# Two of the four sums of weight quarters in each feed-forward block: from VectorE and GpSimd to accumulating DMAs

## The chip, the cores and the metric

The kernel runs on one core of a Trainium2 chip. The metric is the device time of one execution in microseconds (us), the median of three. TensorE (PE) multiplies matrices, VectorE (DVE) and ScalarE (ACT) work on tiles in the on-chip memory, GpSimd (POOL) does so more slowly, and SyncE (SP) issues the loads. Each engine takes its instructions in the order in which the program lists them.

## The reference

A transformer encoder of four layers on one sequence of 512 tokens of width 1024, in float32. A layer is an attention of one of three kinds and then a gated feed-forward part; what is changed stands in the latter:

```
def swiglu(h, w_gu, w_out):
    gu = h @ w_gu
    return (jax.nn.silu(gu[..., :FFN_DIM]) * gu[..., FFN_DIM:]) @ w_out

for i in range(DEPTH):
    ...
    x = x + mix
    x = x + swiglu(rms_norm(x, ffn_norm[i]), f_w_gu[i], f_w_out[i])
```

FFN_DIM is 2816, which is 22 tiles of 128 columns.

## The kernel before

Each float32 matrix is split into a high and a low part (`split`: ACT copies the high part, DVE subtracts it from the source), and a product is three matmuls: high by high, high by low, low by high (`mm3`). In each layer's feed-forward part (`ffn`) the first 4 of the 22 column tiles are computed as they are (`whole`); the other 18, four times 18 = 72 in the kernel, are **blocks** of a fast scheme for 2 by 2 blocks (`quartered`): the activations are combined once per layer (`quarters`), and of the weights of a block four quarters a11, a12, a21, a22 (each 128 partitions by 512 elements, 256 KB) are loaded, from which four sums are made,

    s1 = a21 + a22,   s2 = a11 + s1,   s4 = a12 + s2,   s3 = a11 + a21

so that seven products of 12 matmuls each (256 columns) take the place of eight. The program makes them in the order 5, 2, 1, 3, 6, 7, 4; product 5 reads s1, 3 reads s4, 6 reads s2 and 7 reads s3. Products 1, 3, 6, 7 and 4 build up in three PSUM tiles; after products 1, 6, 7 and 4 DVE takes an intermediate sum out of PSUM (`tmp<-b,tmp`, 128 by 256), and the next product into the same tile waits for that.

Where things lie: the buffer `raw` has eight quarters, 0 to 7. s1, s4, s2, s3 of every block lie in quarters 3, 4, 5 and 6: there is one set of them, used by one block after the other. The loaded a11, a12, a22, a21 of an even block lie in quarters 0, 1, 2 and 7 of `raw`, those of an odd one in `rt` (two), `acc` and `rb`. The split parts have two sets of buffers: even blocks use `whi`, `wlo`, odd ones for the sums `g` and for a11, a12, a22 `whi`, `wlo` as well. In DVE's rows the split of s1 and s4 is the first `128x1024` of a block that reads `raw` (its high part is made by ACT), the split of s2 and s3 is the second; when the first is over, quarters 3 and 4 are free for the next block.

Between the blocks' products PE multiplies the hidden tiles of the phase before by the down weights (matmuls of 512 columns on `xh`, `xl` or `s`; two output tiles a block).

What sets the order: nothing is issued by hand. `Plan` records every operation with a cost and a lag, `run` makes twelve list schedules of the whole program, and the best one fixes the order of the instructions on each engine. The hardware then goes through these fixed orders and waits where an operand is not there. All loads are issued by SP through one queue (`dma`, line 406).

Of the kernel before, what the change touches and what calls it, by code (L numbers as in the profile page):

```python
# [10 lines left out]
ALU = mybir.AluOpType  # L11
# [9 lines left out]
FFN = 2816  # L21
# [157 lines left out]
class Plan:  # L179
# [222 lines left out]
    def dma(self, out, in_, nbytes):  # L402

        nc = self.nc
        val = lambda s: s.ap() if isinstance(s, View) else s
        return self.op("sp", max(475.0, nbytes / 359.0), lambda: nc.sync.dma_start(out=val(out), in_=val(in_)),
                       [in_] if isinstance(in_, View) else [], [out] if isinstance(out, View) else [],
                       lag=2000.0)

# [146 lines left out]
class Net:  # L558
# [272 lines left out]
    def quartered(self, ring, wg, f, xq, sets):  # L831


        p = self.p
        raw = self.raw.buf
        q = lambda b, n, c=1: Region(b, 512 * n, [128, 4 * c, 128])

        if f % 2:
            a21, a22, a11, a12 = q(self.rb, 0), q(self.acc, 0), q(self.rt, 0), q(self.rt, 1)
            plain = [(0, 2, q(self.rt, 0, 2)), (2, 1, a22)]  # L840
        else:
            a21, a22, a11, a12 = q(raw, 7), q(raw, 2), q(raw, 0), q(raw, 1)
            plain = [(0, 3, q(raw, 0, 3))]
        s1, s4, s2, s3 = (q(raw, n) for n in range(3, 7))
        for v, half, c0 in ((a21, 0, FFN), (a22, 1, FFN), (a11, 0, 0), (a12, 1, 0)):
            src = wg[512 * half:512 * (half + 1), c0 + 128 * f:c0 + 128 * (f + 1)].rearrange("(k p) m -> p k m", p=128)
            p.dma(v.all, src, 1 << 18)
        (ha, la), (hb, lb) = sets

        def split(h, l, at, n, src):  # L850
            v = slice(4 * at, 4 * (at + n))
            p.act(h[:, v, :], src.all)
            p.tt(l[:, v, :], src.all, h[:, v, :].bits(F32), ALU.subtract)

        p.tt(s1.all, a21.all, a22.all, ALU.add)
        p.tt(s2.all, a11.all, s1.all, ALU.add)
        p.tt(s4.all, a12.all, s2.all, ALU.add)
        split(hb, lb, 0, 2, q(raw, 3, 2))
        for at, n, src in plain:
            split(ha, la, at, n, src)  # L860
        p.tt(s3.all, a11.all, a21.all, ALU.add, eng="pool")
        split(hb, lb, 2, 2, q(raw, 5, 2))

        place = {1: (ha, la, 0), 2: (ha, la, 1), 4: (ha, la, 2), 5: (hb, lb, 0), 3: (hb, lb, 1), 6: (hb, lb, 2), 7: (hb, lb, 3)}
        n = slice(0, T // 2)
        x, y, z = (self.psum(ring)[:, n] for _ in range(3))
        c1, c2 = slice(0, T // 2), slice(T // 2, T)

        def product(n, out, first):
            h, l, at = place[n]  # L870
            for k in range(NT):
                self.mm3(out, h[:, 4 * at + k, :], l[:, 4 * at + k, :], *xq[n, k], first and k == 0, k == NT - 1, more=not first)

        s, o, t, u = self.tmp.new([128, T]), self.tmp.new([128, T]), self.tmp.new([128, T]), self.tmp.new([128, T // 2])
        product(5, y, True)
        p.act(t[:, c2], y)
        product(2, x, True)
        p.act(t[:, c1], x)
        product(1, z, True)
        p.tt(s[:, c1], z, t[:, c1], ALU.add)  # L880
        product(3, y, False)
        p.act(u.all, y)
        product(6, z, False)
        p.tt(s[:, c2], z, u.all, ALU.add)
        p.act(s.all, s.all, ACTF.Silu)
        product(7, z, False)
        p.tt(o[:, c2], z, t[:, c2], ALU.add)
        p.tt(o[:, c2], o[:, c2], s[:, c2], ALU.mult)
        product(4, z, False)
        p.tt(o[:, c1], z, s[:, c1], ALU.mult)  # L890
        return o
# [752 lines left out]
```

## Time and profile before

| | |
|---|---|
| median of 3 runs | 2734.08 us (2733.46 to 2734.75) |
| the profiled execution | 2733.77 us, of which its span (first to last instruction) 2732.0 us |
| PE busy | 2703.5 us, 99% of the span |
| DVE, ACT, POOL busy | 73%, 51%, 23% |
| granted TensorE clock, mean | 0.997 of full speed |
| read from HBM | 230.66 MB |

Busy shares are averages over attention and feed-forward parts. "Idle before" in a row is the time that the engine waited ahead of an instruction, with what ended the wait.

### The profile page before, as it was taken

What the parts mean: (1) busy time and instruction counts of PE and PEld (TensorE: products, weight loads), DVE (VectorE), ACT (ScalarE), POOL (GpSimd) and SP (SyncE); (2) the same over time, 40 slices, a digit from 0 to 9 for tenths busy, and PEclk for the clock granted to TensorE, in tenths of its full rate; (3) what the DMA queues carried; (4) which work ended last, traced back from release to release, by engine and by line L of the source; (5) the groups of instructions that cost most, each with busy time, mean ns of one, the idle gap of its engine ahead of it and who ended that gap; (6) DMA issues with size and microseconds to landing.
All of it is one profiled execution on the core that took longest, in us unless ns stands there. A gap on an engine that the chain in (4) does not pass through costs nothing.

```text
span 2732.0 us, 43805 instructions
## 1 busy us (share of the span) xinstructions
PE 2703.5 (99%) x16757; PEld 2330.3 (85%) x16757; DVE 1983.5 (73%) x3599; ACT 1382.0 (51%) x2577; POOL 619.3 (23%) x462
## 2 busy tenths in 40 slices
PE   8999999999999999999999999999999999999999
PEld 6778899997777899988888888889998778889998
DVE  7876897756666887765767585688776778688774
ACT  5555444445874544445454545454444555454442
POOL 2432211003642211021312122221101433211001
PEclk9999999999999999999999999999999999999999
DMA  4222343332112343232232322324323212224322
GB/s 145 64 69 62 93 127 106 93 88 60 43 55 86 93 123 93 86 110 80 71 79 63 94 71 79 98 85 120 97 81 117 70 39 81 86 86 117 104 74 66
DMA packets 474975, 235.79 MB, mean 86 GB/s; under 512 B 47935, under 2 KB 471694, under 8 KB 474766
## 3 DMA queue, kind: packets, MB, share of 16 engines
q1 hardware_dynamic: 474766, 233.00, 29.8%
q8 instruction: 131, 2.15, 0.3%
q14 instruction: 78, 0.64, 0.1%
HBM read 230.66 MB, written 2.29 MB: 85 GB/s over the span
## 4 chain that ended last, share of the span: by engine, by line
PE 95%; DVE 2%; ACT 1%; DMA 1%; issue 0%; POOL 0%; SPq 0%; DVEq 0%; POOLq 0%; ACTq 0%
PE b L261 86%; PE b L304 4%; PE b L282 2%; PE b L271 2%; PE b L293 0%; ACT s L328 0%; DVE tmp L341 0%; DVE s L341 0%; DMA raw<-in_a_w_qkv 0%; DVE wlo L341 0%; DVE raw L341 0%; DVE tmp L396 0%; DVE tmp L352 0%; ACT tmp L328 0%; DMA s<-in_x 0%
## 5 line engine op out<-in xcount | busy, mean ns | idle before, releaser
L261 PE MATMUL b<-s,whi 128*128 128x256 f32 (+1 forms) x4000 | 869.4, 313 | 3.5 <-ACT s L328 1.4
L261 PEld LDWEIGHTS b<-s,whi 128*128 128x128 f32 x4000 | 662.1, 191 | 57.6 <-issue 2.1
L261 PE MATMUL b<-s,wlo 128*128 128x256 f32 (+1 forms) x2000 | 623.6, 312 | 0.9 <-DVE wlo L341 0.9
L328 ACT ACTIVATE whi<-raw 128x1024 fp32r<-128x1024 f32 (+4 forms) x350 | 367.0, 1054 | 333.0 <-PE b L261 226.9
L341 DVE TENSOR_TENSOR wlo<-raw,whi 128x1024 fp32r<-128x1024 f32 (+2 forms) x330 | 446.1, 1360 | 73.4 <-ACT whi L328 69.7
L261 PE MATMUL b<-xh,whi 128*128 128x512 f32 x1072 | 434.3, 405 | 3.0 <-DVE tmp L341 2.2
L261 PE MATMUL b<-xh,wlo 128*128 128x512 f32 x1072 | 418.9, 391 | 0.0
L261 PE MATMUL b<-xl,whi 128*128 128x512 f32 x1072 | 418.4, 390 | 0.0
L261 PEld LDWEIGHTS b<-s,wlo 128*128 128x128 f32 x2000 | 381.1, 191 | 22.9 <-DVE wlo L341 1.5
L341 DVE TENSOR_TENSOR tmp<-b,tmp 128x256 f32<-128x256 f32 (+1 forms) x297 | 128.2, 432 | 249.1 <-PE b L261 210.7
L328 ACT ACTIVATE tmp<-b 128x256 f32<-128x256 f32 (+2 forms) x301 | 126.3, 429 | 334.3 <-PE b L261 281.1
L261 PEld LDWEIGHTS b<-xh,whi 128*128 128x128 f32 x1072 | 201.6, 188 | 56.8 <-issue 11.2
L261 PEld LDWEIGHTS b<-xh,wlo 128*128 128x128 f32 x1072 | 201.4, 188 | 43.7
L261 PEld LDWEIGHTS b<-xl,whi 128*128 128x128 f32 x1072 | 201.9, 188 | 36.4
L341 POOL TENSOR_TENSOR tmp<-tmp,rt 128x512 f32<-128x512 f32 x83 | 118.9, 1434 | 491.4 <-DVE tmp L396 457.1
L261 PE MATMUL b<-s,g 128*128 128x256 f32 x1728 | 227.3, 283 | 0.0
L261 PEld LDWEIGHTS b<-s,g 128*128 128x128 f32 x1728 | 220.5, 191 | 5.7
L261 PE MATMUL b<-xh,s 128*128 128x512 f32 x512 | 175.1, 391 | 0.0
L341 POOL TENSOR_TENSOR acc<-acc,tmp 128x512 f32<-128x512 f32 (+1 forms) x56 | 92.9, 1660 | 357.0 <-ACT tmp L328 356.6
L341 POOL TENSOR_TENSOR raw<-raw 128x512 f32<-128x512 f32 x36 | 56.5, 1570 | 440.4 <-DVE g L341 371.3
L379 DVE TENSOR_REDUCE col<-b 128x1 f32<-128x512 f32 x192 | 126.6, 684 | 36.2 <-PE b L261 21.0
L328 ACT ACTIVATE s<-b,col 128x512 f32<-128x512 f32 x196 | 133.3, 687 | 34.7 <-DVE col L379 22.8
(187 smaller groups left out, 4586.4 us busy)
## 6 DMA issues: line engine op xcount, KB each, us to landing
raw<-in_f_w_gu SPq DMA_DIRECT2D x144, 256.0 KB, 3.3
raw<-in_c_w_qkv SPq DMA_DIRECT2D x72, 512.0 KB, 3.8
s<-in_f_w_out SPq DMA_DIRECT2D x128, 256.0 KB, 2.8
raw<-in_a_w_qkv SPq DMA_DIRECT2D x48, 512.0 KB, 3.5
rt<-in_f_w_gu SPq DMA_DIRECT2D x72, 256.0 KB, 3.2
raw<-in_f_w_gu SPq DMA_DIRECT2D x32, 512.0 KB, 4.0
raw<-in_f_w_out SPq DMA_DIRECT2D x32, 384.0 KB, 3.1
acc<-in_f_w_gu SPq DMA_DIRECT2D x36, 256.0 KB, 3.2
```

Source lines behind the costliest of these rows:

```text
L261: nc.tensor.matmul(out.ap(), l.ap(), r.ap(), start=s, stop=e, skip_group_check=more)
L271: nc.tensor.matmul(out.ap(), l.ap(), r.ap(), start=s, stop=e)
L282: nc.tensor.matmul(out.ap(), l.ap(), r.ap(), start=s, stop=e)
L304: nc.tensor.transpose(out.ap(), i.ap(), idn.ap())
L328: nc.scalar.activation(out.ap(), in_.ap(), func, **k)
L341: o = self.op(eng, cost, lambda: e.tensor_tensor(out=out.ap(), in0=a.ap(), in1=b.ap(), op=alu), [a, b], [out])
L379: return self.op("dve", (a.n + 148) / 0.96, lambda: nc.vector.tensor_reduce(out=out.ap(), in_=a.ap(), op=ALU.max, axis=AX, negate=True), [ ...
```

## The change

s1 and s3 are no longer made by DVE and POOL. The first summand is loaded straight into the quarter of the sum (a21 into s1's, a11 into s3's), and a DMA that POOL issues adds the second one to it where it lies (a22 to s1, a21 to s3). a21 and a11 are still loaded into their old places as well, since s3's addition reads a21 and the splits and s2 read a11. So a block has six loads in place of four and two accumulating DMAs.

```
+    def dma_add(self, out, in_):
+
+        nc = self.nc
+        o = self.op("pool", 1100.0, lambda: nc.gpsimd.dma_start(out=out.ap(), in_=in_.ap(), accum_op=ALU.add), [in_, out], [out], lag=3000.0)
+        o.port = True
+        return o
...
         s1, s4, s2, s3 = (q(raw, n) for n in range(3, 7))
-        for v, half, c0 in ((a21, 0, FFN), (a22, 1, FFN), (a11, 0, 0), (a12, 1, 0)):
+
+        for v, half, c0 in ((s1, 0, FFN), (a22, 1, FFN), (a11, 0, 0), (a12, 1, 0), (a21, 0, FFN), (s3, 0, 0)):
...
-        p.tt(s1.all, a21.all, a22.all, ALU.add)
+        p.dma_add(s1.all, a22.all)
         p.tt(s2.all, a11.all, s1.all, ALU.add)
         p.tt(s4.all, a12.all, s2.all, ALU.add)
         split(hb, lb, 0, 2, q(raw, 3, 2))
         for at, n, src in plain:
             split(ha, la, at, n, src)
-        p.tt(s3.all, a11.all, a21.all, ALU.add, eng="pool")
+        p.dma_add(s3.all, a21.all)
         split(hb, lb, 2, 2, q(raw, 5, 2))
```

The instructions of the feed-forward parts are ordered anew on every engine, PE included; in the attention parts the order is the same as before but for a few rows next to the feed-forward parts.

The first place is DVE in the first layer's feed-forward part, from the end of the even block f = 12 (its `tmp` and `x` rows read `b_4119` and `b_4150`) into the odd block f = 13 (`b_4304`). Before:

```order
L341 TENSOR_TENSOR wlo_94<-raw_92,whi_93 128x1024
L341 TENSOR_TENSOR raw_92<-rb_193,acc_194 128x512
L341 TENSOR_TENSOR tmp_4051<-b_4119,tmp_4264 128x256
L341 TENSOR_TENSOR tmp_4051<-tmp_4051,tmp_4083 128x256
L341 TENSOR_TENSOR wlo_94<-raw_92,whi_93 128x1024
L341 TENSOR_TENSOR s_3917<-s_3894,s_3895 128x512
L341 TENSOR_TENSOR tmp_4051<-b_4119,tmp_4083 128x256
L341 TENSOR_TENSOR x_89<-x_89,b_4150 128x512
L341 TENSOR_TENSOR raw_92<-rt_192,raw_92 128x512
```

`raw_92<-rb_193,acc_194` is s1 of block 13: it stands right behind the split that frees its quarter, and its two summands have buffers of their own. The last row is its s2; s4 comes five rows later. The same place now (here the block 12's tiles are `b_4171`, those of block 13 `b_4322`):

```order
L341 TENSOR_TENSOR tmp_4057<-b_4171,tmp_4080 128x256
L341 TENSOR_TENSOR wlo_94<-raw_92,whi_93 128x1024
L341 TENSOR_TENSOR wlo_94<-raw_92,whi_93 128x1536
L341 TENSOR_TENSOR xl_3303<-tmp_4057,xh_3302 128x512
L341 TENSOR_TENSOR s_3954<-s_3945,s_3953 128x512
L341 TENSOR_TENSOR x_89<-x_89,b_4196 128x512
L341 TENSOR_TENSOR wlo_94<-raw_92,whi_93 128x1024
L341 TENSOR_TENSOR tmp_4237<-b_4322,tmp_4420 128x256
L341 TENSOR_TENSOR wlo_94<-rt_192,whi_93 128x1024
L341 TENSOR_TENSOR raw_92<-rt_192,raw_92 128x512 x2
L341 TENSOR_TENSOR tmp_4237<-b_4322,tmp_4450 128x256
L341 TENSOR_TENSOR g_2715<-raw_92,g_2714 128x1024
```

The first row is DVE's work after product 4 of block 12, the second the split of its s1 and s4, which frees the quarters. s1 of block 13 is gone from DVE; s2 and s4 of block 13 (`raw_92<-rt_192,raw_92`, twice) stand between DVE's work after product 1 and after product 6 of block 13 itself.

The second place is POOL at the first layer's first blocks (`tmp<-tmp,rb` are multiplications of the tiles that are computed whole). Before, with the s3 sums of an even block (`raw<-raw`) and an odd one (`raw<-rt,rb`):

```order
L341 TENSOR_TENSOR raw_92<-raw_92 128x512
L341 TENSOR_TENSOR tmp_2860<-tmp_2860,rb_193 128x512
L341 TENSOR_TENSOR tmp_3248<-tmp_3248,rb_193 128x512
L341 TENSOR_TENSOR tmp_3315<-tmp_3315,rb_193 128x512
L341 TENSOR_TENSOR tmp_3377<-tmp_3377,rb_193 128x512
L341 TENSOR_TENSOR raw_92<-rt_192,rb_193 128x512
```

Now the accumulating DMAs, two for each block (`raw<-acc` is s1 of an odd block, `raw<-rb` its s3, `raw<-raw` either sum of an even one):

```order
L413 DMA raw_92<-raw_92 128x512 x2
L341 TENSOR_TENSOR tmp_2857<-tmp_2857,rb_193 128x512
L413 DMA raw_92<-acc_194 128x512
L341 TENSOR_TENSOR tmp_3251<-tmp_3251,rb_193 128x512
L341 TENSOR_TENSOR tmp_3325<-tmp_3325,rb_193 128x512
L341 TENSOR_TENSOR tmp_3386<-tmp_3386,rb_193 128x512
L413 DMA raw_92<-rb_193 128x512
```

From there to the end of the part POOL has only these DMAs, in both kernels' places of s3 and in new ones for s1, so each can start when its operands are there.

## Rows read from the trace of the kernel before

**Rows 1.** The page: busy us, share of span, instructions; and TensorE's granted clock

```profile
PE 2703.5 (99%) x16757; PEld 2330.3 (85%) x16757; DVE 1983.5 (73%) x3599; ACT 1382.0 (51%) x2577; POOL 619.3 (23%) x462
PEclk9999999999999999999999999999999999999999
```

**Rows 2.** Windows over the four feed-forward parts from the first block on

```profile
core 0: us, PE busy (x) PEld busy (x) DVE busy (x) ACT busy (x) POOL busy (x), PEclk, DMA share, GB/s
345.00:631.00 286.00, 286.00 (x1929) 264.58 (x1928) 215.76 (x298) 133.29 (x198) 36.88 (x24) 1.00 0.36 102
925.00:1215.00 290.00, 289.63 (x1960) 268.42 (x1964) 219.65 (x308) 134.35 (x199) 37.98 (x23) 1.00 0.36 106
1770.00:2113.00 343.00, 343.00 (x2223) 313.96 (x2222) 266.85 (x373) 163.46 (x242) 48.83 (x29) 1.00 0.34 99
2435.00:2716.00 281.00, 281.00 (x1931) 262.12 (x1930) 202.93 (x294) 123.85 (x184) 34.21 (x22) 1.00 0.31 91
sum 1200.00, PE 1199.63 PEld 1109.08 DVE 905.18 ACT 554.95 POOL 157.89; mean PE 299.91 PEld 277.27 DVE 226.29 ACT 138.74 POOL 39.47
```

**Rows 3.** The raw tile: sums by engine, duration ns min/median/max; landing times

```profile
L341 DVE TENSOR_TENSOR raw<-raw x108: 674/685/1782, 301.4 to 2637.6; 128x512 f32<-128x512 f32 x108
...
L341 POOL TENSOR_TENSOR raw<-raw x36: 1287/1620/2222, 301.5 to 2632.6; 128x512 f32<-128x512 f32 x36
L341 DVE TENSOR_TENSOR raw<-rb,acc x36: 679/693/1784, 336.5 to 2644.7; 128x512 f32<-128x512 f32 x36
L341 POOL TENSOR_TENSOR raw<-rt,rb x36: 1287/1681/2226, 336.6 to 2648.2; 128x512 f32<-128x512 f32 x36
...
DMA to landing us min/median/max: 1.8/3.5/6.0
```

**Rows 4.** Timeline of PE in an odd block: start us, us, instruction

```profile
402.23 1.59 PE L261 MATMUL b<-s,g 128*128 128x256 f32 x12
403.66 0.40 PE L261 MATMUL b<-s,whi 128*128 128x256 f32 x2
...
406.54 1.60 PE L261 MATMUL b<-s,g 128*128 128x256 f32 x12
407.98 0.40 PE L261 MATMUL b<-xh,s 128*128 128x512 f32 x1
...
408.67 1.59 PE L261 MATMUL b<-s,g 128*128 128x256 f32 x12
```

**Rows 5.** Timeline of DVE beside it

```profile
404.86 1.75 DVE L341 TENSOR_TENSOR wlo<-raw,whi 128x1536 fp32r<-128x1536 f32 x1
406.81 0.42 DVE L341 TENSOR_TENSOR tmp<-b,tmp 128x256 f32<-128x256 f32 x1 [0.19 <-PE b L261]
407.15 0.68 DVE L341 TENSOR_TENSOR raw<-rt,raw 128x512 f32<-128x512 f32 x1
407.75 1.22 DVE L341 TENSOR_TENSOR wlo<-rt,whi 128x1024 fp32r<-128x1024 f32 x1
408.88 0.68 DVE L341 TENSOR_TENSOR raw<-rt,raw 128x512 f32<-128x512 f32 x1
```

**Rows 6.** The chain that ended last, 912 to 926 us: start us, us, what

```profile
915.89 1.74 POOL tmp L341
917.63 0.02 issue
917.65 2.84 DMA rb<-in_f_w_gu
...
920.58 0.69 DVE raw L341
```

**Rows 7.** DMA issues: KB each, median us from issue to landing

```profile
raw<-in_f_w_gu SPq DMA_DIRECT2D x144, 256.0 KB, 3.3
...
rb<-in_f_w_gu SPq DMA_DIRECT2D x36, 256.0 KB, 3.0
...
out<-s SPq DMA_DIRECT2D x8, 256.0 KB, 2.3
```

**Rows 8.** Timeline of POOL: an instruction of four elements a partition

```profile
70.57 1.02 POOL L341 TENSOR_TENSOR col<-col,lam 128x4 f32<-128x4 f32 x1 [20.64 <-DVE col L365]
```

**Rows 9.** Timeline of SP's queue: the issue of one load

```profile
403.79 0.37 SPq L406 DMA_DIRECT2D rb<-in_f_w_gu  x1
```

**Rows 10.** DMA queue, 345 to 560 us: packets, MB, share of 16 engines' time

```profile
q1 hardware_dynamic: 43371, 21.54, 34.7%
```

**Rows 11.** PE's waits over the whole span: us in total, times, longest us

```profile
PE b L304 <- DVE s L352: 6.8, 4, 2.1
...
PE b L261 <- DVE wlo L341: 0.9, 3, 0.5
```

## The prediction

> **What bounds the kernel now.** I read the page first: PE is busy for 2703.5 of 2732.0 us, at the full clock nearly throughout [rows 1]. The other engines are far from that, so what is taken from DVE and POOL counts only where PE waits for them. The change lies in the four feed-forward parts alone, so I looked at those by windows: over the four stretches of blocks, 1200 us together, PE is busy for 1199.63 [rows 2], and of PE's waits for a split weight the whole trace has 0.9 us, in three pieces [rows 11]. The other 27 us of idle PE lie in the attention parts and at the two ends (the longest group of waits is for attention's tiles, [rows 11]), where the order stays. So about 1.3 us is all that the best possible change of the sums can win here, and the question is only whether it makes PE wait.
>
> **What it removes.** DVE loses 72 sums of about 0.69 us (36 `raw<-rb,acc` and 36 of the 108 `raw<-raw`), 50 us; POOL loses 72 of about 1.65 us, 119 us [rows 3]. Worth in time: nothing, since PE's matmuls cover both. DVE is busy for 905 of the 1200 us [rows 2], 75%, and falls to about 71%.
>
> **What it adds.** 144 loads of 256 KB on SP (0.37 us of issue each, [rows 9]), 37.7 MB. A load takes the 16 DMA engines 0.91 us: 34.7% of 215 us for 21.54 MB, which are 82 loads [rows 10]. With eight loads for six in 15.6 us and two additions of at least as much each, the share goes from 0.35 to about 0.6: no bound, but loads may queue a little longer. Then 144 accumulating DMAs on POOL, which has little else to do there.
>
> **What it moves** is the point. Before, both summands of s1 had buffers of their own and were there long before; s1 followed right behind the split that frees its quarter, as the first order of rows in the section on the change shows. Now, from the end of that split, a load must land in the quarter, POOL must add to it, and only then may DVE make s2. s2 stands in DVE's fixed order among the sums out of PSUM for which PE waits. Behind a late s2 they queue, and PE with them.
>
> *The chain.* A load, from the end of the instruction that frees its buffer to the start of DVE's instruction that reads it: 917.63 to 920.58, 2.9 us [rows 6]; the median to landing is 3.0 for such a load [rows 7]. I call L the time from the landing to the start of s2: the accumulating DMA with its issue. The trace has none. From below: 256 KB out of the on-chip memory in rows of 512 elements land after 2.3 us on SP's queue [rows 7]. Nearest is the 2.9 us load, changed in two things: POOL's shortest instruction, 1.02 us [rows 8], takes the place of SP's issue of 0.37 [rows 9], which makes 3.55; and a second operand is read, which at most doubles the 0.91 us on the engines, 4.45. I take 4.0, the middle. From above: POOL's part stretched as its sums are at worst beside DVE (2226 for 1287 ns, [rows 3]), 1.02 to 1.76, and the slowest landing of the tile `raw`, 6.0 [rows 3], less SP's 0.37: 7.4 us.
>
> *What the order allows.* I worked this out for the odd block 13 of the first layer, whose order is shown. PE's pace: 12 matmuls of 256 columns take 1.44 us (402.23 to 403.66), three of 512 take 0.69 (407.98 to 408.67) [rows 4]. With time 0 at the start of the even block 12, PE's order gives products 5, 2, 1, 3 to 5.75, three matmuls of 512, product 6 to 7.88, six of 512, product 7 to 10.72, six, product 4 to 13.55, nine, and block 13 starts at 15.64. DVE starts 0.27 us after PE's end (product 1 ends at 406.54, DVE at 406.81, [rows 4, 5]); in a row its instructions come 0.34 us apart for 256 elements (406.81 to 407.15), 0.60 for 512 and 1.13 to 1.15 for 1024 (407.75 to 408.88) [rows 5]. So DVE's sum after product 4 runs from 13.82 to 14.18, the split of s1 and s4 to 15.33, and the quarters are free. The load lands in DVE's sense at 18.3. In block 13 product 6 ends at 15.64 + 7.88 = 23.52, and product 7 wants to start at 15.64 + 9.28 = 24.92. Before it DVE must have done s2, s4 and the sum after product 6 (0.60 + 0.60 + 0.36, and 0.1 for the signal): s2 must start by 23.25. So L may be 23.25 − 18.3 = 4.9 us here, 0.9 more than I take.
>
> I made the same sum for the other blocks, from the order of the changed kernel and the same durations. The allowance is 4.9 in three blocks (13 of layers 1, 3 and 4), under 5.5 in 8 of 71, under 6.0 in 17, under 7 in 21, under 8 in 47; the tight ones are the middle blocks of each part, and the longest allowances (9 to 16) stand in the first ones. PE's wait is the sum of what L exceeds them by: nothing at L = 4.0 and 4.5, 0.2 us at 5, 2 at 5.5, 9 at 6, 18 at 6.5, 28 at 7, 41 at 7.5, 60 at 8, 112 at 9. The pieces add up, since every block's anchors are PE's own. s3 is harmless: its addition is needed for the second split alone, which comes about a block later.
>
> The sum: 2733.77 (the profiled execution: span 2732.0 and 1.77 around it, 0.3 under the median of 2734.08) − 0 to 1.3 + 0 = about 2733.5; against the median, **2734 us**.
>
> **Rivals.** (1) *The addition is slower than the allowance* (other side). The wait moves from PE's weights to DVE, which stands before s2 with PE's sums behind it; from L of 5.7 on it shows (5 us). For it: POOL's sums take 1620 to 1681 ns in the median against 1287 alone [rows 3], so POOL is held up by DVE, which is busy three quarters of the time; if an addition's descriptors have to wait until two of DVE's instructions are over, 1.75 and 0.69 us [rows 5], L is 4.0 + 2.4 = 6.4 and the cost 16 us, 2750. At my upper end, 7.4, it is 38 us, 2772. Against it: what stretches POOL's sums is that both engines read operands at once, and an addition moves its data on the DMA engines. The Trainium skill (SBUF — State Buffer, box on the "DVE blocks DMA" trap) says that a DMA issued by GpSimd is starved of descriptors while VectorE, in a mode that takes both ports, holds the one that they share, and gives about 620 ns alone and 3100 beside a float32 copy of that kind. An estimate by that page adds 2.5 us to L and comes out at 2751, if DVE's sums of two operands held the port as such a copy does. No row of this trace has such a DMA. Chance 0.26.
>
> (2) *The loads come later.* With eight loads a block in one queue, s1's lands behind others. The loads into `raw` already take 3.3 us in the median where those into `rb` take 3.0 [rows 7], and 6.0 at the slowest [rows 3]. Every tenth shortens all allowances; a landing after 5 us acts like 2 us more of L, 9 us at L = 4.0: 2743, and only at 4.7 us does it begin to show. Chance 0.07.
>
> (3) *A gain.* The first odd block's s1 no longer waits for `rb`, which stood in the chain ahead of 925 us [rows 6]. But PE's waits there are those 0.9 us [rows 11]; 2733. More than 5.5 us would have to come from attention, whose order stays. Chance of that 0.03.
>
> **How the numbers follow.** A difference of 0.2%, 5.5 us, is about what a measurement of this kernel can tell. No change, L up to 5.7, from 2732 to 2739: 0.64. Slower, rivals 1 and 2: 0.33. Faster: 0.03. The likeliest is no change, 2734. For the range I reach to L = 7.3, 36 us: 2770, which leaves about 0.1 above, and down to 2731, 3 us under the sum, which leaves 0.03.
>
> **What would show it.** Right: 144 accumulating issues on POOL with about 3.5 to 5 us to landing, DVE's and POOL's busy time down by some 50 and 119 us, HBM reads up by 37.7 MB, and PE as full in the four stretches as it is. Wrong: rows of waits of DVE's `raw` for the additions of 1 us and more in the middle blocks, with PE waiting for DVE's `tmp` behind them; the more, the further the landing is over 5 us. It would also be wrong if a block that I count as loose stalls because SP, in order, has an unready load ahead of s1's.

## The result and the profile after

The kernel became slower: 2767.39 us (median of 4 runs, 2764.01 to 2769.38) against 2733.77 (4 runs beside them), a ratio of 1.012, 95% interval 1.0108 to 1.0133. That is 33.6 us more, six times the 0.2% that a measurement can tell. The profiled execution took 2769.17 us, with a span of 2767.4.

From the page of the changed kernel, the lines that answer to [rows 1] and [rows 10]:

```profile
PE 2712.6 (98%) x16757; PEld 2329.7 (84%) x16757; DVE 1902.3 (69%) x3527; ACT 1377.7 (50%) x2577; POOL 624.4 (23%) x534
...
q1 hardware_dynamic: 550798, 270.76, 34.5%
q0 software_dynamic: 20736, 37.76, 8.0%
...
HBM read 268.41 MB, written 2.29 MB: 98 GB/s over the span
```

PE has the same 16757 matmuls and is without work for 54.8 us of its span; before it was 28.5. DVE is busy for 81 us less. POOL looks as busy as before only because the page counts the 144 new issues there (0.87 us each, 125 us in all). The new queue q0 holds the additions: 37.76 MB, and 8.0% of the 16 engines' time for them, while q1 takes 34.5% for 270.76 MB.

The windows over the four feed-forward parts, moved with the delay so that they hold about the work of [rows 2]:

```profile
core 0: us, PE busy (x) PEld busy (x) DVE busy (x) ACT busy (x) POOL busy (x), PEclk, DMA share, GB/s
347.00:641.00 294.00, 288.36 (x1924) 265.68 (x1927) 198.52 (x278) 132.07 (x198) 39.82 (x39) 0.99 0.61 155
935.00:1232.00 297.00, 292.35 (x1964) 268.51 (x1962) 201.38 (x290) 133.53 (x199) 39.66 (x39) 1.00 0.63 161
1787.00:2137.00 350.00, 346.56 (x2224) 314.77 (x2222) 245.40 (x355) 162.78 (x242) 49.72 (x47) 1.00 0.59 151
2459.00:2751.00 292.00, 282.85 (x1928) 261.65 (x1928) 186.12 (x277) 124.14 (x186) 35.00 (x37) 1.00 0.57 144
sum 1233.00, PE 1210.12 PEld 1110.61 DVE 831.43 ACT 552.52 POOL 164.20; mean PE 302.53 PEld 277.65 DVE 207.86 ACT 138.13 POOL 41.05
```

The stretches are 33 us longer, 1233 for 1200, and PE is no longer full in them. The DMA share rose from 0.35 to 0.6, as forecast.

Both kernels run the same number of matmuls, and 15732 of the 16757 stand under the same names (buffer numbers left out) at the same place in PE's order. So the start of the n-th one can be compared with the n-th one before, and where the difference grows over many matmuls, time is lost. By layers it grows by 10.4, 6.4, 6.8 and 12.0 us, 35.6 together, inside the feed-forward parts and hardly anywhere else (less than 1 us in any attention part). Within a part nearly all of it comes by the middle; the last five of the 18 blocks lose next to nothing. I use this count below and call it the loss by matmuls.

What PE waited for, from the view of waits (total us, times, longest us):

```profile
DVE raw L341 <- DMA raw<-raw: 45.6, 24, 4.3
...
PEld b L261 <- DVE tmp L341: 37.6, 29, 3.0
...
DVE raw L341 <- DMA raw<-acc: 35.4, 17, 4.9
...
PE b L261 <- DVE tmp L341: 26.5, 24, 2.6
```

These are the rows that the prediction named as proof against it. DVE's `raw` (s2) stands still 41 times for an addition, 81 us in all, and PE's two queues wait for DVE's `tmp` behind it; before, PEld waited 5.4 us for `tmp`. The additions themselves, from the view of their line (ns min/median/max, and us to landing):

```profile
L413 POOL DMA_DIRECT2D raw<-raw x72: 854/869/1058, 291.9 to 2671.5; - x72
L413 POOL DMA_DIRECT2D raw<-acc x36: 854/868/895, 315.2 to 2683.4; - x36
L413 POOL DMA_DIRECT2D raw<-rb x36: 859/876/1075, 337.1 to 2687.3; - x36
...
DMA to landing us min/median/max: 3.2/4.2/7.7
```

The chain that ended last, through blocks 12 and 13 of layer 1; block 13 is the one that the prediction worked out (start us, us, what):

```profile
425.30 3.20 DMA raw<-in_f_w_gu
...
429.17 4.18 DMA raw<-raw
...
433.43 0.70 DVE raw L341
...
438.14 0.58 DVE wlo L341
...
441.60 6.33 DMA raw<-acc
...
448.02 0.70 DVE raw L341
...
449.36 0.43 DVE tmp L341
...
449.83 16.23 PE b L261 x101
```

The first three rows are block 12's load, addition and s2. In block 13, the split of s1 and s4 that frees the quarters ended at 438.06, s1's load was issued at 438.09 and landed at 440.9, POOL issued the addition at 441.60, and it took 6.33 us to land. s2 and the `tmp` behind it followed, and PE started only then. In 16 of the 72 blocks of the changed kernel the split of s2 and s3 comes ahead of that of s1 and s4 (in 11 before the change), so the first `128x1024` of a block is not always the one that frees s1's quarter. Block 11 of layer 1 is such a block, and the load at 425.30 waited for its second split. SP's queue shows what else was under way in those microseconds:

```profile
438.09 2.77 SPq L406 DMA_DIRECT2D raw<-in_f_w_gu  x3
441.13 0.37 SPq L406 DMA_DIRECT2D s<-in_f_w_out  x1
441.55 1.68 SPq L406 DMA_DIRECT2D raw<-in_f_w_gu  x2
```

### The profile page after: what moved, and what is told of

Read it like the earlier page. It is cut to its first block, busy times and chain, and to the rows that moved or that the text cites. A ratio compares the mean times of both kernels' runs of the same rounds, so it can differ in the third digit from the quotient of the medians.

```text
span 2767.4 us, 44333 instructions
## 1 busy us (share of the span) xinstructions
PE 2712.6 (98%) x16757; PEld 2329.7 (84%) x16757; DVE 1902.3 (69%) x3527; ACT 1377.7 (50%) x2577; POOL 624.4 (23%) x534
## 3 DMA queue, kind: packets, MB, share of 16 engines
q1 hardware_dynamic: 550798, 270.76, 34.5%
q0 software_dynamic: 20736, 37.76, 8.0%
## 4 chain that ended last, share of the span: by engine, by line
PE 85%; DMA 6%; DVE 5%; issue 2%; ACT 1%; POOL 0%; SPq 0%; POOLq 0%; DVEq 0%; ACTq 0%
PE b L261 76%; PE b L304 4%; PE b L282 2%; PE b L271 2%; DMA raw<-acc 2%; DMA raw<-raw 2%; DMA raw<-in_f_w_gu 1%; DVE tmp L341 1%; DVE wlo L341 1%; DVE raw L341 1%; DMA raw<-rb 1%; DVE s L341 0%; ACT s L328 0%; PE b L293 0%; DVE g L341 0%
## 5 line engine op out<-in xcount | busy, mean ns | idle before, releaser
L413 POOL DMA_DIRECT2D raw<-raw x72 | 63.0, 882 | 440.4 <-DVE tmp L341 127.5
```

What stands on the lines that cost most here:

```text
L413: o = self.op("pool", 1100.0, lambda: nc.gpsimd.dma_start(out=out.ap(), in_=in_.ap(), accum_op=ALU.add), [in_, out], [out], lag=3000.0)
```

## The experiments

Theory A says that the chain of load and addition is longer than the order leaves room for. Theory B says that the second loads and the additions crowd the DMA engines, so that everything lands late. The us are medians, with the median of the kernel before on the same chip and the ratio's 95% interval.

| kernel | us | before | ratio |
|---|---|---|---|
| 1 s1 alone by DMA | 2752.09 | 2735.44 | 1.0057 (1.0044 to 1.0069) |
| 2 s3 alone by DMA | 2745.42 | 2735.44 | 1.0036 (1.0023 to 1.0048) |
| 3 second loads, no additions | 2742.80 | 2735.44 | 1.0030 (1.0018 to 1.0042) |
| 4 planner's lag 5000 | 2743.95 | 2735.44 | 1.0035 (1.0023 to 1.0048) |
| 5 s2, s4 on POOL | 2792.53 | 2734.87 | 1.0213 (1.0199 to 1.0227) |
| 6 copies for additions | 2742.47 | 2734.87 | 1.0026 (1.0017 to 1.0035) |
| 7 as 3, loads of 64 KB | 2734.93 | 2734.87 | 1.0000 (0.9991 to 1.0009) |
| 8 as 4, first two blocks old | 2742.62 | 2734.87 | 1.0027 (1.0017 to 1.0037) |
| 9 both lags | 2766.88 | 2735.23 | 1.0115 (1.0101 to 1.0129) |
| 10 additions of 64 KB | 2741.25 | 2735.23 | 1.0022 (1.0013 to 1.0031) |
| 11 s1 alone, lag 5000 | 2739.05 | 2735.23 | 1.0015 (1.0007 to 1.0024) |
| 12 both lags, last four blocks old | 2743.10 | 2735.50 | 1.0026 (1.0016 to 1.0036) |
| 13 loads of 64 KB, full additions | 2746.98 | 2734.62 | 1.0044 (1.0031 to 1.0058) |
| 14 as 12, first two blocks old too | 2737.37 | 2734.62 | 1.0012 (1.0003 to 1.0020) |

**1 and 2, one sum each.** The other sum goes back to DVE or POOL, and its second load with it.

```diff
-        p.dma_add(s3.all, a21.all)
+        p.tt(s3.all, a11.all, a21.all, ALU.add, eng="pool")
```

> Only s1 is made by an accumulating DMA (72 second loads, 72 adds); s3 is a POOL sum again. Theory A (the chain: split end, load 3.0 us, 0.7 us to the POOL issue, 4.2 us to the landing, about 8 us against some 7.8 that the order leaves, and DVE's tmp sums queued behind s2): most of the loss stays, 2755 to 2770 us, and PE's two queues wait for DVE tmp 20 to 40 us. Theory B (the second loads and the adds crowd the DMA engines): half of that traffic is gone and so is about half of the loss, 2745 to 2755.

> Only s3 is made by an accumulating DMA; s1 is a DVE sum again. Theory A: s3's landing is ahead of the split that reads it by 1 to 8 us in the changed kernel, and no DVE sum waits for it, so 2733 to 2738 us. Theory B: half of the traffic, so about half of the loss, 2745 to 2755.

s1 alone costs 16.7 us and s3 alone 10.0, 26.7 together for 33.6. So s3 is not free, as A had it, and s1 falls a little short of what A asked. By their ranges both kernels lie in B's 2745 to 2755. That PE's two queues wait 34.6 us for DVE's `tmp` in kernel 1 is what A asked for. In s3's kernel 7.2 of 9.6 us by matmuls are lost in layer 2 alone, 4.4 of them from 922 to 932 us. ACT's timeline there:

```profile
916.65 0.62 ACT L328 ACTIVATE s<-tmp 128x512 fp32r<-128x512 f32 x1
921.43 0.63 ACT L328 ACTIVATE xh<-s 128x512 fp32r<-128x512 f32 x1 [4.16 <-DMA s<-in_f_w_out]
921.97 0.61 ACT L328 ACTIVATE tmp<-tmp 128x512 f32<-128x512 f32 x1
```

ACT stands 4.16 us at a quarter of f_w_out and has its `tmp` behind it, for which POOL, DVE and PE wait in turn. The load was issued at 915.50, right after three loads into `raw` from 913.80 on, and took 5.9 us. That is B's way of losing time, and no addition stands in this chain.

**3 and 7, the second loads without additions.**

```diff
-        p.dma_add(s1.all, a22.all)
-        p.dma_add(s3.all, a21.all)
 # kernel 7 also
-            p.dma(v.all, src, 1 << 18)
+            if v is s1 or v is s3:
+                p.dma(v[:, 0:1, :], src[:, 0:1, :], 1 << 18)
+            else:
+                p.dma(v.all, src, 1 << 18)
```

> Both accumulating DMAs are left out and the second loads stay, so s1 is a21 alone and s3 is a11 alone; the traffic of SP's queue is that of the changed kernel, the chain is the load's 3 us and no add. Theory A: 2732 to 2738 us, DVE raw waits no more. Theory B: the loads are half of the added traffic, 2745 to 2760.

> The kernel with the second loads and no additions, in its own order, but each second load brings 64 KB in place of 256, so s1 and s3 are a quarter true. Theory B' (the 7.4 us of that kernel are crowding: 37.7 MB more that the loads of f_w_out and of the tight blocks land behind): 2733 to 2738 us and s<-in_f_w_out lands in 2.8 to 3.0 us again. Rival (the wait for any load at that place, or the new order): 2740 to 2745.

The two kernels have one order on every engine, and differ in bytes alone: 7.4 us with 256 KB, 0.1 with 64. So it is the bytes of the second loads that cost. Most of it looks like crowding, B's part: some 5 of the 7.4 us arise where the chain that ended last runs through loads of f_w_out, which DVE and ACT wait for beside the chain of s1. But a short load also lands sooner itself (64 KB after 1.9 us in the median), and DVE's s2 waited 20.7 us for loads into `raw` in kernel 3 and 7.7 in kernel 7; the two kernels don't separate that part. Kernel 7, which makes s1 and s3 by neither sums nor additions, also shows that taking the sums away gains nothing and that an order made anew need not cost anything. Kernel 3's chain, beside one of its stalls:

```profile
363.00 4.27 DMA s<-in_f_w_out
367.29 0.64 ACT xh L328
...
369.25 0.35 DVE tmp L341
...
369.64 1.46 PE b L261 x10
```

A quarter of f_w_out lands after 4.27 us; its median over the kernel is 3.3 us, 3.0 in kernel 7, 2.8 before and 3.8 in the changed kernel.

**4, the planner is told 5000 ns.** Nothing changes but a number by which the order is made.

```diff
-        ... [in_, out], [out], lag=3000.0)
+        ... [in_, out], [out], lag=5000.0)
```

> The whole change, but the planner is told 5000 ns instead of 3000 from the end of an add's issue to its landing, 6.1 us with the issue. Theory A: DVE's order then leaves the chain room and puts tmp sums ahead of s2, so at most a third of the loss stays, 2733 to 2745 us. Theory B: the traffic is the same, so the time is too, above 2755.

25 of the 33.6 us go, with all loads and additions in place, as A had it. The line's view in this kernel:

```profile
who waited for it (us, times):
  DVE raw L341: 6.4, 7
...
DMA to landing us min/median/max: 3.1/3.6/6.0
```

DVE now waits 6.4 us for additions in place of 81. From the split's end to the landing the chain is as long as it was (median 8.0 us, 8.1 in the changed kernel); s2 merely stands later in the order, 9.8 us after the split in place of 8.5.

**5, s2 and s4 on POOL.**

```diff
-        p.tt(s2.all, a11.all, s1.all, ALU.add)
-        p.tt(s4.all, a12.all, s2.all, ALU.add)
+        p.tt(s2.all, a11.all, s1.all, ALU.add, eng="pool")
+        p.tt(s4.all, a12.all, s2.all, ALU.add, eng="pool")
```

> The whole change, with s2 and s4 put on POOL (144 POOL sums of 1.3 to 1.7 us), so that it is POOL that waits for s1's addition and DVE's tmp sums have no unready sum ahead of them. Theory A (what costs is DVE's queue standing behind s2): half of the loss or more goes, 2735 to 2750 us, and PE waits for DVE tmp no more than 10 us. Rival C (what costs is the weights being late themselves, the split of s1 and s4 after the chain): the chain is 2 us longer by POOL's slower sums and the time is 2765 or more, with PE waiting for wlo.

The opposite of what theory A expected: 57.7 us slower, a time that rival C allowed. Its waits:

```profile
ACT whi L328 <- POOL raw L341: 53.3, 23, 5.6
...
ACT g L328 <- POOL raw L341: 49.4, 16, 7.5
...
PEld b L261 <- DVE tmp L341: 28.8, 22, 3.6
...
PEld b L261 <- ACT tmp L328: 18.9, 16, 3.3
```

DVE no longer stands at s2, but ACT stands at the splits that read the sums, with its own `tmp` work behind them, and DVE at the halves that need ACT. The sums are slower too (1.30 us in the median for 0.69). So the part of theory A that blamed DVE's place alone falls. That the chain's length against the order counts, whichever queue it stands in, fits this run but is not shown by it, since the order and the length of the sums changed together. PE waited for `tmp` here too, of DVE and ACT, and not for the weights' halves as rival C said.

**6 and 10, what an addition costs over a copy, and its bytes.** Both keep the order of the changed kernel on every engine.

```diff
 # kernel 6
-... in_=in_.ap(), accum_op=ALU.add) ...
+... in_=in_.ap()) ...
 # kernel 10
-        p.dma_add(s1.all, a22.all)
+        p.dma_add(s1[:, 0:1, :], a22[:, 0:1, :])
```

> Order, loads and queues of the changed kernel, word for word; the 144 POOL DMAs copy instead of accumulating, so s1 is a22 and s3 is a21. Theory D (the accumulation itself, which also reads what it writes, makes the landing long): landing falls from a median of 4.2 us by 1 us or more, DVE raw waits 20 us or less in place of 81, and the time is 2740 to 2750. Rival E (the landing is the fixed cost of a DMA issued from POOL and of queueing): landing 3.9 to 4.2 us and 2760 to 2770 us.

> Order, loads and queues of the changed kernel; each addition adds 64 KB of its 256, so s1 and s3 are summed in a quarter of their elements. If the extra microsecond of an accumulating DMA over a copying one is work on the bytes, the landing falls to 2.5 us or less, and with it the 25 us: 2736 to 2744, what the second loads alone cost. If it is a fixed cost of an accumulating DMA, the landing stays at 3.3 us or more and the time is 2745 to 2760.

With copies 26 of the 33.6 us are gone, and 28 with a quarter of the bytes. Kernel 6's queues and its line:

```profile
q0 software_dynamic: 11520, 37.76, 3.5%
...
DMA to landing us min/median/max: 2.2/3.1/5.2
```

The same 37.76 MB take 3.5% of the engines in place of 8.0, and land 1.0 us sooner at the least and 1.1 in the median; DVE's `raw` waits 19.6 us for them in place of 81. Since the engines have less to do as well (a quarter of f_w_out lands after 3.5 us in the median in place of 3.8), these 26 us are not the chain's alone; kernel 4 is the run that keeps all the traffic. For kernel 10 the answer of that line is:

```profile
DMA to landing us min/median/max: 2.3/3.0/5.5
```

A quarter of the bytes lands as soon as a full copy. So most of the extra microsecond is work on the bytes, not a fixed price of accumulating. The 2.5 us or less that I expected holds for the fastest only; I take the rest of the 3.0 us for queueing, which no run shows by itself.

**13, the fourth corner.** Kernel 7's edit of the loads, with the additions in full and the changed kernel's order of instructions.

> Order, queues and full additions of the changed kernel; each second load brings 64 KB of its 256, so s1 and s3 are sums in which three quarters of one summand are stale. If the additions alone pass what the order leaves (the theory that the loss is their extra microsecond): 2755 to 2765 us. If the chain has a fixed allowance and the load's share of it counts as much (64 KB land in 1.9 us, 1.2 us sooner): the addition's wait shrinks as with the copying DMA, and the time is 2734 to 2742.

Neither guess: 12.4 us. Put as a square, in us over the kernel before:

```
                        second loads 256 KB   second loads 64 KB
additions                     33.6                 12.4
copies (left), none (right)    7.6                  0.1
```

The lower right corner is kernel 7, which has no copies and an order of its own; the other three share the changed kernel's order. 7.6 and 12.4 make 20, and together they cost 33.6. That fits two parts of one chain that spend the same allowance: what either uses up leaves the other the less.

**8, 9, 11, 12 and 14, which order gives it back.** 8 and 14 keep the old sums (`p.tt`, single loads) in the first two blocks of each layer, 12 and 14 in the last four. 8, 9, 11, 12 and 14 have the addition's lag at 5000; 9, 12 and 14 also tell the planner that the quarters' loads take longer, and 9 says the same of f_w_out's loads.

```diff
-            p.dma(v.all, src, 1 << 18)
+            p.dma(v.all, src, 1 << 18).lag = 3500.0
```

> Planner's lag 5000 as in the fourth kernel, and the first two blocks of each layer make s1 and s3 by DVE and POOL sums, as before the change. What stayed of the loss there was 9 us by the matmuls' times, 5 to 6 of them within the first two blocks' stretch of layers 2 and 4, where an addition waits in POOL's queue for a late load of rb and POOL's tmp product stands behind it. If that is so: 2735 to 2740 us. Rival (crowding by the second loads alone): 2741 to 2745.

> The whole change with the planner's lag of the addition at 5000 ns, as in the fourth kernel (2744 us), and that of the FFN's loads at 3500 in place of 2000. If the 7 to 9 us that stayed are loads which land later than the order allows, and an order can make room for them as it did for the additions, the time is 2734 to 2738 us. Rival (crowding cannot be planned away, since each load frees a buffer that the next one needs): 2741 to 2746.

> Only s1 by an accumulating DMA, as in the first kernel (2752 us), with the planner's lag 5000. The chain's part of that kernel's 17 us goes and half of the second loads stays: 2736 to 2741 us. Rival (the chain costs even with room in the order): 2745 or more.

> As the kernel with both lags (addition 5000, the quarters' loads 3500; f_w_out's loads back at 2000), but the last four blocks of each layer make s1 and s3 by DVE and POOL sums from single loads. That kernel's matmuls ran without a gap from 345 to 570 us and lost 4 to 10 us at each stretch's end, where its last s2 stands some 216 PE rows later than in the changed kernel and the loads of f_w_out that need the raw tile come late. If this is all that it lost: 2733 to 2740 us, with no step of over 2 us at the four ends. Rival (the chain with room slips later in every block, and a loss returns elsewhere): 2745 or more.

> As the kernel with the old sums in the last four blocks, and in the first two blocks of each layer as well; 12 of 18 blocks keep the additions, with both lags told. By the matmuls' times the kernel before it lost 1.3 to 3.3 us in the first blocks of layers 2, 3 and 4 and nothing elsewhere. If that is all: 2734 to 2738 us. Rival (the loss is spread over the blocks with second loads, wherever they are): 2740 to 2744.

Kernel 11 gave what was asked: with room, s1 alone costs 3.8 us. Kernel 8 missed: 7.8 us stay, so the first blocks alone were not what was left at a lag of 5000. Nor was it POOL's queue, as I had written there; kernel 4's chain in the first blocks of layer 2 has the late quarter of f_w_out that kernel 2 has, 5.74 us from 914.08 on. Kernel 9 missed badly, and its windows in layer 1 say where:

```profile
345.00:570.00 225.00, 225.00 (x1572) 210.91 (x1571) 150.74 (x225) 102.81 (x152) 25.41 (x29) 1.00 0.67 167
570.00:640.00 70.00, 67.34 (x386) 58.91 (x384) 44.25 (x57) 31.94 (x47) 16.10 (x10) 0.98 0.50 129
```

For 225 us, at a DMA share of 0.67, PE is as full as before the change, so an order can make room for this traffic. But the blocks now fall further and further behind (s2 comes 11 us later than in the changed kernel in block 12 and 21 us in block 21, the last), and the last split ends so late that the loads of f_w_out which need the raw tile miss their time. Its chain there:

```profile
592.87 1.15 DVE g L341
...
594.03 3.94 DMA raw<-in_f_w_out
```

Kernel 12, without the change in the last four blocks and with f_w_out's lag back at 2000, has no such loss in layer 1. Which of the two did it, no run separates:

```profile
345.00:570.00 225.00, 225.00 (x1568) 210.71 (x1568) 160.78 (x233) 101.42 (x155) 28.14 (x27) 1.00 0.60 153
570.00:640.00 70.00, 70.00 (x403) 61.15 (x402) 43.45 (x53) 32.90 (x51) 14.35 (x9) 1.00 0.41 109
```

It missed its 2733 to 2740 by 3 us all the same; by matmuls it lost 3.1, 4.1 and 1.7 us in the other three layers, most of it in their first blocks. Kernel 14 takes those out as well, keeps the change in 12 of 18 blocks, and stands at 2737.37, 2.75 us or 0.12% over before: less than the 0.2% that I count as a difference, though the interval of 0.03% to 0.20% leaves a small loss. No version gained, as PE's full stretches before the change had said.

## Why the prediction was wrong

The forecast was 2734, no change; the measured 2767.4 lies in the range, on the side that had 0.33. What happened is rival 1 in its form (the wait moves to DVE, before s2, with PE's sums behind it), but not by its mechanism. That the time is near its upper price, 2772, is luck: that price belongs to an L of 7.4 us in every block, and the measured middle of L, 5.0, costs 0.2 us by the prediction's own sums. Two steps failed, and a third term had no price.

**The first step that failed is the value of L.** I set one typical 4.0 us for all blocks against each block's allowance. Measured from the load's landing, L is 0.7 us until POOL's issue starts (a part I had no term for) and then 3.2 to 7.7 us, 4.3 in the median, for the 64 blocks from the third of each layer on. So the middle of L was short by 1.0, and the spread was worse. From the split's end to the addition's landing these blocks took 7.2 to 12.0 us, 8.1 in the median; my 2.9 and 4.0 made 6.9. A loss that begins at a threshold is made by the long ones, and a middle value says nothing of it. I had 6.0 and 7.4 us as the slow ends, and used them for the range alone.

**The allowances were about right for a block by itself.** With them and each block's measured chain, the working of the prediction picks out the blocks that stalled (us; the allowance is that for L plus 3.0 for the load; the loss is by matmuls around s2, good to some 0.4 us):

```
layer, block   allowance   chain measured   over   PE lost
1, 13             7.9           9.9          2.0     4.4
2, 13            10.1          11.6          1.5     2.6
3, 13             7.9          10.1          2.1     4.7
4, 13             7.9          10.2          2.3     3.0
1, 16            10.8          11.8          1.1     1.4
4, 16            10.8          12.0          1.3     1.7
4, 12             8.4           8.1          0       2.0
all               -             -           12.2    35.6
```

Block 13 was the example of the prediction. But the excesses make 12.2 us of 35.6.

**The second step that failed is "The pieces add up, since every block's anchors are PE's own".** They are not. s2 and the split that frees the quarters for the next block stand in one order on DVE. Where s2 is late and PE does not wait yet, the split becomes late too, and the next block starts its chain with less room. Kernel 6 has the same order on every engine and shorter chains, so its trace tells where that split belongs against PE's matmuls. In layer 1 the split that starts the chain of blocks 9, 10, 11 and 12 comes 0.2, 0.3, 1.0 and 1.6 us later against them than in kernel 6. Block 12's own chain only just reaches its allowance (8.1 us, against some 8), and yet PE waits 1.65 us:

```profile
434.51 0.50 PE L261 MATMUL b<-s,whi 128*128 128x256 f32 x2 [1.65 <-DVE tmp L341]
```

In block 12 of layers 2, 3 and 4 the split is 1.6, 1.7 and 1.8 us late. With allowances taken from kernel 6's trace the excesses of the chains alone make some 13 us, as in the table; with what each block inherits they make some 21, and PE's stalls at the sums that follow s2 make 22. This is read from the two traces; no run changes it alone.

**The sign that the prediction named last came true as well.** In blocks 16 of layers 1 and 4 SP, in order, stood at a load that was not ready, ahead of s1's. In layer 1:

```profile
482.19 0.37 SPq L406 DMA_DIRECT2D rb<-in_f_w_gu  x1
482.65 1.01 SPq L406 DMA_DIRECT2D rt<-in_f_w_gu  x2
483.76 3.63 SPq L406 DMA_DIRECT2D raw<-in_f_w_gu  x2
```

The load of `rb` for block 17 had to wait until s3's addition in block 15, which reads `rb`, landed at 482.17. The split that frees block 16's quarter ended at 482.43, but the load into s1's quarter left at 483.76 only, behind two more loads.

The rest, about 14 us, is known in part. Behind the stalls of block 13 in layers 1 and 3 the granted clock fell. In layer 1 PE had been busy for 12.71 of 15 us, and in the next 15 the granted clock is 0.89 of the full 2.4 GHz, a mean of its two levels (2.4 and 1.2), which takes 1.65 us:

```profile
435.00:450.00 15.00, 12.71 (x90) 11.61 (x89) 11.03 (x16) 6.88 (x11) 1.15 (x2) 1.00 0.55 141
450.00:465.00 15.00, 15.00 (x94) 13.85 (x95) 9.05 (x14) 6.60 (x11) 2.37 (x3) 0.89 0.78 192
```

In layer 3 ten-microsecond windows have 0.96 and 0.87, 1.7 us. Blocks 5 of layers 1 and 4 lost about 1.6 us each to s3, whose addition of `rb` in the first odd block was waited for by ACT. My sum supposed every other instruction on time, and s1's chain is not the only one that crowding makes late. For the 7 us or so that are left I can't name the place.

**"Loads may queue a little longer" had no price.** It was put at nothing (rival 2, 0.07, would have been 9 us). Kernels 3 and 7 give 7.4 us for the bytes of the second loads alone. That the share of the DMA engines stays at 0.6 is true, and no comfort: a quarter of f_w_out lands after 3.8 us in the median in place of 2.8. The slowest load into `raw` whose landing the trace tells took 6.5 us, 6.0 before [rows 3].

**"s3 is harmless"** was wrong: 10.0 us in kernel 2, with half of the second loads in it. Nearly half of that is one late load of f_w_out, and in the changed kernel block 5's wait for the addition of `rb` is another piece. I had asked who reads s3's sum, and not what its load and addition push back in the queues, SP's among them.

**Rival 1's mechanism** was POOL held up by DVE. It wasn't: the issues took 854 to 1075 ns beside a DVE that is busy two thirds of the time. The 2.5 us that the prediction estimated for it rested on an if: that DVE's sums of two operands hold POOL as a copy does. The Trainium skill (SBUF — State Buffer, box on the "DVE blocks DMA" trap) says so of a mode that a float32 copy takes, not of such sums; this trace agrees, since no issue was stretched beyond 1075 ns. What made L long was the accumulation, 1.1 us in the median by kernel 6, and the spread of the landings.

**What held.** There was nothing to gain with PE full, and taking DVE's and POOL's sums away is worth nothing in time: kernel 7, without those of s1 and s3, stands at 2734.93 us against 2734.87. HBM reads rose by 37.7 MB; the place of the wait, and the views that would show it, were as written. A slip that changes nothing: PE's idle time outside the four stretches is 28.1 us and not 27 (28.5 less 0.37).

## What to carry to other kernels

Where a wait is set against an allowance that a fixed order leaves, take the whole chain from release to reader with each hand-over in it, and ask for the slow landings as well as the middle one: the price is made by the blocks that exceed theirs. Ask too whether a late block starts the next one late: here that took the sum of the excesses from some 13 to some 21 us. Two changes that spend the same allowance can cost more than their sum, 33.6 us for 7.6 and 12.4. Where a planner makes the order, tell it the measured time of a new operation; here 3000 against 5000 ns in one number was worth 25 us, while giving more room to the loads as well let the work slip until the end of the part missed its time. Taking work off an engine that the bound engine does not wait for was worth nothing here, and what replaced it brought a wait.

## What the hardware showed that was not expected

- An accumulating DMA of 256 KB from on-chip memory to on-chip memory, issued from POOL, lands after 3.2 us at the least and 4.2 in the median, a copying one in the same place of the same order after 2.2 and 3.1. It takes 2.3 times the time of the DMA engines (8.0% against 3.5%, in 20736 packets against 11520). The Trainium skill (DMA: Bandwidth & Descriptors, section on the anatomy of a DMA from GpSimd) fits 2.0 us and a term for the bytes, an estimate of 2.6 us for 256 KB. The copies lie on both sides of that, at 2.2 to 5.2 us; the additions all lie above it.
- From the landing of the load that it waits for to the start of POOL's issue pass 0.7 us in the median and 1.0 at most, in the 29 blocks whose landing the trace tells (from the third of each layer on).
- DVE lost 81 us of busy time and not 50. Its sums into `raw` went from 160.9 to 100.1 us, of which 55 are the 72 sums that are gone; the rest is instructions that got shorter, such as `raw<-rt,raw`, 756 ns in the mean before and 702 after. POOL's sums are the likely reason: in kernel 2, where DVE keeps its s1 and POOL's sums are gone, the 36 `raw<-rb,acc` take 690 ns in the mean, and 802 before.
